# Retention read-out in wide banks, stacked up-projections, grouped transposes and solve, and another order of first loads, in a two-layer hybrid trunk on one core

## Chip, cores and metric

The kernel runs on one core of a Trainium2 chip. The metric is the device time of one execution in microseconds (us), taken as the median of several runs. Beside it there is one execution recorded by the hardware profiler, with the start, the duration and the releaser of each instruction on each engine: PE (TensorE, matmuls and transposes), DVE (VectorE), ACT (ScalarE), POOL (GpSimd), SP (SyncE, which only issues transfers) and the DMA queues.

## What is computed

A decoder trunk of two layers over 512 positions and 1024 channels in float32. In each layer a normalised input is projected at once for three branches and their gates; the branches are merged, projected and added; then comes a gated feed-forward with a causal convolution of width 3.

```python
for l in range(2):
    h = rmsnorm(x, norm1_g[l]);  p = h @ w_in[l]
    p_rw, p_ret, p_sg, gate_logits = split(p, ...)
    # RWKV-7, 8 heads of 64: decay and rate come from two products of rank 64
    w = -softplus(-(w0 + tanh(wd) @ w_up)) - 0.5;  decay = exp(-exp(w));  a = sigmoid(a0 + ad @ a_up)
    S_t = S_{t-1} (diag(decay_t) - kk_t^T (a_t kk_t)) + v_t^T k_t;   y_t = S_t r_t     # then norm, gate
    # retention, 4 heads, 4 chunks of 128, q and k rotated by (cos, sin)
    y_n = (q_n k_n^T * decay_in) v_n + (q_n * q_dec) R_n;  R_{n+1} = R_n chunk_decay + (k_n * k_dec)^T v_n
    y_ret = y / rms(y per head) * silu(g)
    # spatial gating: z = gelu(p_sg), halves u, v;  y_sg = u * (tril(w_s) @ layernorm(v) + b_s)
    x = x + (sum_i sigmoid(gate_i) * (y_i @ w_branch[l, i])) @ w_out[l]
    x = x + conv_ffn(rmsnorm(x, norm2_g[l]))
return rmsnorm(x, final_g)
```

## The kernel before

**Products.** Nearly all work is matmuls of 128x128 weights against 512 columns. A float32 operand is split into two parts of type float32r: hi, a copy on ACT, and lo, what is left, a subtraction on DVE (L127 and L128 for weights, L136 and L137 in `split`). A product is then three matmuls, hi·lo, hi·hi and lo·hi (`mm3`, L144 is its one call of PE). Weights arrive in units of 128x512 (256 KB): `load` issues on SP, `part` splits, and a plan made in a first pass over the program says which unit is next, so that the split runs 2 to 5 units ahead (`AHEAD`). Small products of the branches stay in plain float32.

**Memory.** Tiles of 128x512 come from pools of fixed size in turn: 31 `u`, 16 `r`, 39 `f` (opened in the mixer's second half), and in PSUM two sets of four banks, `acc` for the bulk products and `sm` for everything else. Whoever asks for a fifth `sm` bank waits until the first has been read.

**Order.** The program is emitted in one order and then scheduled; an instruction passed to `keep_in_program_order` (`po`) keeps its place on its engine against the others so marked. Work that is free to be anywhere is held in `fillers`: gates, then the retention's projections `ret_proj`, then half of the gating block's. `fill(n)` emits the next n steps of it, 12 matmuls for a gate's step. `FILL = (33, 3, 1)`: 33 steps ahead of the solve's matmuls, 3 at the start of each of its two groups, 1 at each pause of the recurrence.

**Start (`run`).** All 250 columns of parameters of layer 1 (`load_pc`, 125 KB of them on ACT's queue by the page) are loaded first; then eight blocks of x on SP's queue (two on ACT's), with three weight units between; then a hand-written string of steps: `z` scales and splits a block (L202, L203), `w` splits a weight, `s` squares a block for the norm.

**RWKV (`rwkv`).** `col` finishes a projected row block; `prep(m)` prepares one of four head pairs. In it, L441 multiplies the 64 rows of `w_up` and the 64 rows of `a_up` (both in one tile `wua`, split in hi and lo) by the two halves of `wa`: three matmuls of 64 rows for each, 48 in both layers. `solve` inverts 32x32 triangles: DVE works by rows, then PE makes z (L686) and pt (L694) for the off-diagonal blocks, 16 blocks at a time in two groups, each z copied by ACT (L689) before its pt. L649 and L651 are long diagonal copies on ACT and POOL. The recurrence goes over eight chunks: `vpair` and L551 transpose, L561 and L564 make y and x, L565 and L566 copy x (`XB`), L572 and L574 update, L576 copies on DVE, L581 and L583 finish, L589 or L591 form the next state, which POOL scales (L595). Between the parts stand single filler steps.

**Retention.** In `ret_proj`, run as filler beside the recurrence, each 128 positions of q and k are scaled (L710) and rotated by five DVE operations: one of 512 columns (L716), two products of 256 (L717, L718), a difference and a sum (L719, L720). `ret_heads` transposes them; `ret_chunk(c)` makes scores (L769), masks (L771), read-out (L777, L780) in two banks of two heads each, the mean square of each pair of heads (L786 on DVE, root on POOL in L789), the row scaling (L792), then the next state R (L799 to L807). `ret_out` transposes and splits the result (L815).

**Second half of the mixer.** `sgu_v`, `rwkv_out` and `sgu_bias` run first; L856 sums the masked weights over rows by a float32 matmul with ones. Then comes a hand-written string of steps (L332): S is a gating group (`sgu_out`), R a `ret_chunk`, U two more filler-like steps of the gating projection, Y `ret_out`, and 0, 1, 2 are merges of 12 bulk matmuls each for the three branches (`merge`, L876 to L882; the sum of two branches lies on POOL for 2, on DVE for 1).

**End (`finish`).** The last 256-row weight is multiplied for two halves of 256 positions; for each half the norm's root (POOL) is spread by two transposes (L988), and eight DVE operations of 256 columns (L994) make the output, sent by SP and ACT in turn.

Of the kernel before, what the change touches and what calls it, by code (L numbers as in the profile page):

```python
# [8 lines left out]
F32 = mybir.dt.float32  # L9
# [9 lines left out]
NC = 4  # L19
# [4 lines left out]
FILL = (33, 3, 1)  # L24
# [22 lines left out]
class Emit:  # L47
# [210 lines left out]
    def run(self):  # L258
# [4 lines left out]
        self.ones = self.cp.tile([128, 128], F32, name="ones")  # L263
        V.memset(self.rst, 1.0)
        V.memset(self.ones, 1.0)
        nc.scalar.copy(self.small((128, 1), "ms"), self.rst[:, 0:1])
        wu = self.acc()
        for i in range(6):
            nc.tensor.matmul(wu[:, 0:256], self.rst[:, 0:128], self.rst[:, 256:512], start=True, stop=True)
        self.load_pc(0)  # L270
# [3 lines left out]
        with tc.high_priority():  # L274
            for j in range(8):
# [3 lines left out]
        for step in "z0 w z1 z2 w z3 w z4 z5 w z6 z7 w s0 s1 s2 w s3 s4 s5 s6 s7".split():  # L279
# [9 lines left out]
        self.keep = False  # L289
        tc.keep_in_program_order(nc.scalar.dma_start(self.con, a["con"]))  # L290
# [17 lines left out]
    def mixer(self, l, nst):  # L308
# [20 lines left out]
        self.ret_heads()  # L329
        self.pool = "r"  # L330
        rest, chunk = self.sgu_u(l, range(2, 4)), iter(range(NC))
        for step in "S S 0 0 R U S 0 R 0 U S 0 0 R 0 0 R 2 2 Y 2 1 2 1 2 1 2 1 2 1 2 1 1 1".split():  # L332
            if step == "S":
                ysg.append(self.sgu_out(len(ysg)))
            elif step == "R":
                self.ret_chunk(next(chunk))
# [47 lines left out]
    def rwkv(self, l, nst):  # L384
# [5 lines left out]
        V.tensor_scalar(omu, pcol("mu", 14), -1.0, 1.0, op0=MUL, op1=ADD)  # L390
# [26 lines left out]
        A.activation(wa[0:64, :], wa[0:64, :], AF.Tanh)  # L417
        Xh, Xl = self.split(wa)
# [13 lines left out]
        def prep(m):  # L432
# [5 lines left out]
            for i in range(3):  # L438
                w, x = (Wh, Wh, Wl)[i], (Xl, Xh, Xh)[i]
                for ks, o in ((slice(64, 128), pA), (slice(0, 64), pL)):  # L440
                    T.matmul(o, w[ks, ms], x[ks, :], start=i == 0, stop=i == 2)  # L441
# [99 lines left out]
        for c in range(8):  # L541
# [25 lines left out]
            self.fill(FILL[2], True)  # L567
# [50 lines left out]
    def rwkv_out(self, l, yT, bv, gd):  # L618
# [3 lines left out]
        for m in range(4):  # L622
            ms = slice(m * 128, m * 128 + 128)
            pt = self.sm()
            for c in range(NC):
                T.transpose(pt[:, c * 128:c * 128 + 128], yT[c][:, ms], self.c("ident"))
# [9 lines left out]
    def solve(self, G, n2):  # L636
# [40 lines left out]
        self.fill(FILL[0])  # L677
        for g in range(2):
            self.fill(FILL[1], g > 0)
            us = range(16 * g, 16 * g + 16)  # L680

            zs = self.r((128, 16, 32), n="zs")
            z = [self.sm((128, 16, 32)) for _ in range(2)]
            for i, u in enumerate(us):
                for h in range(2):
                    po(T.matmul(z[h][(hi, lo)[i % 2][h], i, :], G[lo[h], u, 32:64], TD[lo[h], u, :], start=True, stop=True))  # L686
            for h in range(2):
                for e in range(2):
                    A.copy(zs[hi[h], e::2], z[h][(hi, lo)[e][h], e::2])  # L689
            self.fill(FILL[2], True)  # L690
            pt = [self.sm((128, 16, 32)) for _ in range(2)]
            for i, u in enumerate(us):
                for h in range(2):
                    po(T.matmul(pt[h][(lo, hi)[i % 2][h], i, :], zs[hi[h], i, :], TT[hi[h], u, :], start=True, stop=True))  # L694
            for h in range(2):
                for e in range(2):
                    A.copy(G[lo[h], 16 * g + e:16 * g + 16:2, 32:64], pt[h][(lo, hi)[e][h], e::2])
# [425 lines left out]
```

## Time and profile before

| | |
|---|---|
| median of 3 runs | 1767.47 us (1766.63 to 1768.12) |
| profiled execution, whole | 1764.65 us |
| its span on the core | 1762.9 us |
| PE, DVE, ACT, POOL busy | 99%, 66%, 45%, 10% of the span |

Times in the profile are microseconds from the start of the span unless they are marked ns. `L144` is line 144 of the kernel. A line such as `PE sm L574 <- DVE XB L566: a, b, c` in the view of waits gives how often the engine stood idle for that releaser, the sum and the longest of it. In the chain of waits a line has the start, the duration, engine, tile and line, and how many instructions (`x6`) the piece joins. A line of groups has busy time and mean ns of one, then the idle time of the engine ahead of them by what ended it. In a row of the timeline the idle time ahead of an instruction and its releaser stand in brackets. A view by windows gives its length, then for PE, its weight loads, DVE, ACT and POOL the busy time and count, then the granted TensorE clock, the share of the DMA engines and their GB/s.

### The profile page before, as it was taken

The numbers are of one execution on the slowest core, as the hardware profiler recorded it, in microseconds if no ns is written. First come the engines' busy times: TensorE is split into PE (matmuls) and PEld (weight loads), VectorE is DVE, ScalarE is ACT, GpSimd is POOL, SyncE is SP. The second block draws the span as 40 slices with busy tenths as digits, with TensorE's granted clock in tenths as the row PEclk, the third lists the DMA queues.
The fourth block names the chain that finished last, engine by engine and source line by source line (L and its number), as shares of the span: only waits on it lengthen the run. The fifth ranks groups of instructions, "written<-read, shape, count | busy, mean of one in ns | idle before, by whom it ended". The sixth has DMA issues, their size and how long they took to land.

```text
span 1762.9 us, 26337 instructions
## 1 busy us (share of the span) xinstructions
PE 1745.6 (99%) x9870; PEld 1431.8 (81%) x9870; DVE 1163.1 (66%) x1996; ACT 785.8 (45%) x1349; POOL 174.6 (10%) x206
## 2 busy tenths in 40 slices
PE   9999999999999999999999999999999999999998
PEld 7878877888888888888887787778887888888887
DVE  6887746468668777753358876465776687777433
ACT  6564454543244444343245545445332454443321
POOL 0132011013300000000002220110132000000000
PEclk9999999999999999999999999999999999999999
DMA  4224432314442222243322343324154422321332
GB/s 169 78 91 142 140 109 79 123 66 164 161 141 93 97 100 97 68 122 113 111 87 72 117 141 122 104 79 140 60 167 139 150 95 97 100 97 63 111 98 82
DMA packets 104111, 193.30 MB, mean 110 GB/s; under 512 B 11952, under 2 KB 16304, under 8 KB 103984
## 3 DMA queue, kind: packets, MB, share of 16 engines
q1 hardware_dynamic: 89280, 159.42, 28.1%
q10 hardware_dynamic: 10224, 17.52, 2.9%
q0 software_dynamic: 4480, 14.68, 2.5%
q8 instruction: 78, 1.28, 0.3%
q14 instruction: 49, 0.40, 0.1%
HBM read 174.80 MB, written 16.78 MB: 109 GB/s over the span
## 4 chain that ended last, share of the span: by engine, by line
PE 96%; DVE 2%; issue 1%; ACT 1%; DMA 0%; POOLq 0%; POOL 0%; DVEq 0%; ACTq 0%
PE acc L144 88%; PE sm L485 1%; PE sm L441 1%; PE sm L561 0%; PE sm L864 0%; PE sm L780 0%; PE sm L769 0%; PE sm L452 0%; PE sm L564 0%; PE sm L572 0%; PE sm L581 0%; DMA x<-xT 0%; PE sm L144 0%; PE sm L777 0%; PE sm L551 0%
## 5 line engine op out<-in xcount | busy, mean ns | idle before, releaser
L144 PE MATMUL acc<-lo,sh 128*128 128x512 f32 x1056 | 414.2, 393 | 2.2 <-DVE lo L137 1.2
L144 PE MATMUL acc<-hi,sh 128*128 128x512 f32 x1056 | 413.3, 391 | 0.0
L144 PE MATMUL acc<-hi,sl 128*128 128x512 f32 x1056 | 411.6, 391 | 0.0
L127 ACT CAST sh<-wr 128x512 fp32r<-128x512 f32 x376 | 228.3, 612 | 381.8 <-PE acc L144 287.9
L128 DVE TENSOR_TENSOR sl<-wr,sh 128x512 fp32r<-128x512 f32 x376 | 258.5, 691 | 179.9 <-PE acc L144 97.3
L144 PE MATMUL acc<-lo,wh 128*128 128x512 f32 x640 | 253.1, 396 | 1.7 <-DVE lo L203 1.2
L144 PE MATMUL acc<-hi,wh 128*128 128x512 f32 x640 | 250.4, 391 | 0.0
L144 PE MATMUL acc<-hi,wl 128*128 128x512 f32 x640 | 249.5, 391 | 0.0
L128 DVE TENSOR_TENSOR wl<-wr,wh 128x512 fp32r<-128x512 f32 x208 | 150.5, 724 | 131.2 <-ACT wh L127 127.8
L144 PEld LDWEIGHTS acc<-lo,sh 128*128 128x128 f32 x1056 | 198.3, 188 | 45.0 <-issue 3.2
L144 PEld LDWEIGHTS acc<-hi,sl 128*128 128x128 f32 x1056 | 198.3, 188 | 40.7
L144 PEld LDWEIGHTS acc<-hi,sh 128*128 128x128 f32 x1056 | 198.3, 188 | 40.5
L127 ACT CAST wh<-wr 128x512 fp32r<-128x512 f32 x208 | 128.4, 618 | 225.1 <-PE acc L144 193.1
L144 PE MATMUL acc<-ah,sh 128*128 128x512 f32 (+1 forms) x748 | 219.5, 377 | 0.0
L144 PEld LDWEIGHTS acc<-ah,sh 128*128 128x128 f32 x748 | 137.6, 188 | 25.8
L144 PEld LDWEIGHTS acc<-lo,wh 128*128 128x128 f32 x640 | 120.1, 188 | 29.6 <-DVE lo L203 1.9
L144 PEld LDWEIGHTS acc<-hi,wl 128*128 128x128 f32 x640 | 120.1, 188 | 27.0 <-issue 1.1
L144 PEld LDWEIGHTS acc<-hi,wh 128*128 128x128 f32 x640 | 120.2, 188 | 25.4 <-issue 1.1
L144 PE MATMUL acc<-ah,sl 128*128 128x512 f32 (+1 forms) x374 | 140.8, 376 | 0.0
L915 DVE TENSOR_TENSOR fu<-acc,rsF 128x512 f32<-128x512 f32 x88 | 60.7, 690 | 69.6 <-PE acc L144 69.5
L917 ACT ACTIVATE cv<-fu,pc 128x512 f32<-128x512 f32 x88 | 71.8, 816 | 44.0 <-DVE fu L915 39.3
L144 PEld LDWEIGHTS acc<-ah,sl 128*128 128x128 f32 x374 | 70.4, 188 | 12.8
(279 smaller groups left out, 2166.5 us busy)
## 6 DMA issues: line engine op xcount, KB each, us to landing
wr<-wall SPq DMA_DIRECT2D x488, 256.0 KB, 2.6
wr<-wdn SPq DMA_DIRECT2D x80, 256.0 KB, 2.7
gd<-gth ACTq DMA_DIRECT2D x48, 256.0 KB, 3.3
gth<-gd POOLq DMA_DIRECT2D x48, 256.0 KB, 3.2
tab<-rot ACTq DMA_DIRECT2D x8, 256.0 KB, 3.4
xi<-xT SPq DMA_DIRECT2D x8, 256.0 KB, 3.2
wr<-wdn SPq DMA_DIRECT2D x16, 128.0 KB, 2.1
xd<-xi POOLq DMA_DIRECT2D x8, 256.0 KB, 2.8
```

The lines of the kernel that those rows point to most:

```text
L127: self.kept(self.nc.scalar.copy(hi[:, :n], raw[:, :n]))
L128: self.kept(self.nc.vector.tensor_tensor(lo[:, :n], raw[:, :n], hi[:, :n], op=SUB))
L144: i = self.nc.tensor.matmul(*x, **y)
L441: T.matmul(o, w[ks, ms], x[ks, :], start=i == 0, stop=i == 2)
L485: T.matmul(pgs[h][:, j, :], bk[hv[h], c, :, :].rearrange("p a t -> p (a t)"), ag[hv[h], h, c, :], start=True, stop=True)
L915: V.tensor_tensor(u, ps, self.rsF, op=MUL)
L917: A.activation(t, u, AF.Identity, scale=self.p("cw2", j), bias=self.p("cb", j))
```

## The change

It has eight parts, none of which changes the result that is computed.

- **First loads.** The eight columns of the first norm are loaded alone, into a tile of their own, and the whole parameter block after the first string of steps. In that string the fourth block's scaling stands ahead of the second weight's split. One of six warm-up matmuls goes; `ones` becomes float32r and is a copy.
- **Stacked up-projections.** The host stacks `w_up` and `a_up` each upon themselves, so that a weight tile has hi in rows 0 to 63 and lo in rows 64 to 127; the 64 rows of `wa` are doubled likewise, tanh for one and a POOL copy for the other, and split. Two matmuls of 128 rows take the place of three of 64.
- **Solve.** Both groups' z in one run (64 matmuls, each two rows of the trace), both groups' copies, then `FILL[1]` = 2 steps, both groups' pt; DVE makes half of the copies. `FILL` goes from (33, 3, 1) to (36, 2, 1), and the first chunk of the recurrence has one more step behind `XB`.
- **Rotary.** The two products of 256 columns go from DVE to POOL.
- **Retention.** `ret_chunk` becomes `ret_scores` (scores, mask, next state) and `ret_read` (read-out and norm), each in one bank for four heads; the decayed keys `kd` are made in `ret_heads`. In the string of steps `ret_heads` (H) stands behind a merge, scores (K) and read-out (O) are a step or more apart, three merges of branch 0 stand behind the read-out's last, and two behind Y.
- **Transposes in a row.** Those of `rwkv_out`, `ret_heads`, `ret_out` and the matmuls of `sgu_out`, scores and read-out are kept in program order.
- **Ones matmul.** The masked weights are split, and two float32r matmuls take the place of the float32 one.
- **Last rows.** In the second half, three of eight output blocks are scaled by the gain on ACT ahead of time and by the root on POOL; DVE makes five. The broadcast is first copied by ACT for POOL's use.

```diff
-FILL = (33, 3, 1)
+FILL = (36, 2, 1)
...
-        self.load_pc(0)
+        self.pc = self.sp.tile([128, 64], F32, name="g1", tag="g1", bufs=1)
...
+            tc.keep_in_program_order(nc.scalar.dma_start(self.pc[:, 0:8], a["pcols"][0][:, PC["n1"]:PC["n1"] + 8]))
             for j in range(8):
...
-        for step in "z0 w z1 z2 w z3 w z4 z5 w z6 z7 w s0 s1 s2 w s3 s4 s5 s6 s7".split():
+        tc.keep_in_program_order(nc.scalar.copy(self.small((128, 1), "ms"), self.rst[:, 0:1]))
+        tc.keep_in_program_order(nc.scalar.copy(self.ones, self.rst[:, 0:128]))
+        for step in "z0 w z1 z2 z3 w w z4 z5 w z6 z7 w s0 s1 s2 w s3 s4 s5 s6 s7".split():
...
+        self.load_pc(0)
...
+        self.wsp = self.split(self.ws.rearrange("p g i -> p (g i)"), self.f)
...
-        for step in "S S 0 0 R U S 0 R 0 U S 0 0 R 0 0 R 2 2 Y 2 1 2 1 2 1 2 1 2 1 2 1 1 1".split():
+        for step in "0 H 0 S S K 0 U O K U S O K 0 S O K 0 0 O 2 2 Y 0 0 2 1 2 1 2 1 2 1 2 1 2 1 1 1".split():
...
-        wua = self.u(n="wua")
-        self.tc.keep_in_program_order(nc.scalar.dma_start(wua, a["wua"][l]))
-        Wh, Wl = self.split(wua)
+        Ws = []
+        for i in range(2):
+            wua, s = self.u(n="wua"), self.u(dt=F32R, n="wus")
+            self.tc.keep_in_program_order(nc.scalar.dma_start(wua, a["wua"][l, i]))
+            A.copy(s, wua)
+            P.tensor_tensor(s[64:128, :], wua[64:128, :], s[64:128, :], op=SUB)
+            Ws.append(s)
...
-        A.activation(wa[0:64, :], wa[0:64, :], AF.Tanh)
-        Xh, Xl = self.split(wa)
+        Xs = []
+        for i in range(2):
+            x = self.u(n="wax")
+            for h in range(2):
+                o, s = x[64 * h:64 * h + 64, :], wa[64 * i:64 * i + 64, :]
+                if i == 0:
+                    A.activation(o, s, AF.Tanh)
+                else:
+                    P.tensor_copy(o, s)
+            hi, lo = self.u(dt=F32R, n="hi"), self.u(dt=F32R, n="lo")
+            A.copy(hi, x)
+            P.tensor_tensor(lo, x, hi, op=SUB)
+            Xs.append((hi, lo))
...
-            for i in range(3):
-                w, x = (Wh, Wh, Wl)[i], (Xl, Xh, Xh)[i]
-                for ks, o in ((slice(64, 128), pA), (slice(0, 64), pL)):
-                    T.matmul(o, w[ks, ms], x[ks, :], start=i == 0, stop=i == 2)
+            for o, w, (xh, xl) in zip((pL, pA), Ws, Xs):
+                T.matmul(o, w[:, ms], xl, start=True, stop=False)
+                T.matmul(o, w[:, ms], xh, start=False, stop=True)
...
-            self.fill(FILL[2], True)
+            self.fill(FILL[2] + (c == 0), True)
...
         self.fill(FILL[0])
+        zs = [self.r((128, 16, 32), n="zs") for _ in range(2)]
+        z = [[self.sm((128, 16, 32)) for _ in range(2)] for _ in range(2)]
+        for g, i in [(g, i) for g in range(2) for i in range(16)]:
+            for h in range(2):
+                po(T.matmul(z[g][h][(hi, lo)[i % 2][h], i, :], G[lo[h], 16 * g + i, 32:64], TD[lo[h], 16 * g + i, :], start=True, stop=True))
         for g in range(2):
-            self.fill(FILL[1], g > 0)
...
-                    A.copy(zs[hi[h], e::2], z[h][(hi, lo)[e][h], e::2])
+                    (V.tensor_copy if h else A.copy)(zs[g][hi[h], e::2], z[g][h][(hi, lo)[e][h], e::2])
+        self.fill(FILL[1], True)
+        pt = [[self.sm((128, 16, 32)) for _ in range(2)] for _ in range(2)]
...
-            V.tensor_tensor(b[:, :, 0, :], src[:, :, 1, :], Ss, op=MUL)
-            V.tensor_tensor(b[:, :, 1, :], src[:, :, 0, :], Ss, op=MUL)
+            nc.gpsimd.tensor_tensor(b[:, :, 0, :], src[:, :, 1, :], Ss, op=MUL)
+            nc.gpsimd.tensor_tensor(b[:, :, 1, :], src[:, :, 0, :], Ss, op=MUL)
...
+    def ret_scores(self, c):
+        V, T, po = self.nc.vector, self.nc.tensor, self.tc.keep_in_program_order
+        R, v = self.R, self.vt[c]
+        pS = self.sm((128, 4, 128))
+        for j in range(2):
+            po(T.matmul(pS[:, 2 * j:2 * j + 2, :], self.kF[j][:, c, :], self.qB[j][c // 2][:, c % 2], start=True, stop=True))
+        sc = self.u((128, 4, 128), n="sc")
+        V.tensor_tensor(sc, pS, self.c("rmask").rearrange("p (h i) -> p h i", i=128), op=MUL)
+        self.sc, self.Rc = sc, R
...
+    def ret_read(self, c):
+        nc, V, A, T, po = self.nc, self.nc.vector, self.nc.scalar, self.nc.tensor, self.tc.keep_in_program_order
+        R, v, g, sc = self.Rc, self.vt[c], self.yg[c], self.sc
+        hd = [(j, h) for j in range(2) for h in range(2)]
+        pO = self.sm((128, 4, 128))
+        for j, h in hd if c > 0 else ():
+            po(T.matmul(pO[:, 2 * j + h, :], self.qB[j][c // 2][:, c % 2, h, :], R[:, j, :], start=j == h == 0, stop=False, skip_group_check=True))
+        for j, h in hd:
+            i = 2 * j + h
+            po(T.matmul(pO[:, i, :], sc[:, i, :], v[:, 128 * i:128 * i + 128], start=c == i == 0, stop=True, skip_group_check=True))
+        y = self.u((128, 4, 128), n="ry")
+        A.copy(y, pO)
+        sq = self.u((128, 4, 128), n="rsq")
+        A.activation(sq, y, AF.Square)
+        ss = self.small((128, 4), "rss")
+        V.tensor_reduce(ss, sq, axis=AX.X, op=ADD)
+        V.tensor_scalar(ss, ss, 4.0 / 128, 4e-6, op0=MUL, op1=ADD)
+        rr = self.small((128, 4), "rrr")
+        nc.gpsimd.tensor_tensor(rr, ss, self.c("mhalf")[:, 0:4], op=POW)
+        for i in range(4):
+            o = g[:, 128 * i:128 * i + 128]
+            V.scalar_tensor_tensor(o, y[:, i, :], rr[:, i:i + 1], o, op0=MUL, op1=MUL)
...
-        nc.tensor.matmul(pb, self.ones, ws, start=True, stop=True)
+        for i in (1, 0):
+            nc.tensor.matmul(pb, self.ones, self.wsp[i], start=i == 1, stop=i == 0)
...
+            if gx:
+                pbs = self.u((128, 256), n="pbs")
+                po(A.copy(pbs, pb))
+            order = [j for i in range(4) for j in ((i, i + 3) if i < 3 else (6, 7))] if gx else range(8)
...
+                if gx and j < 3:
+                    nc.gpsimd.tensor_tensor(t, gx[j], pbs, op=MUL)
...
-                (nc.sync if j % 2 else nc.scalar).dma_start(self.a["out"][:, j, hs[h]], t)
+                (nc.scalar if j in (1, 4, 6) else nc.sync).dma_start(self.a["out"][:, j, hs[h]], t)
```

More of the change, by code (lines that the diff above doesn't have):

```diff
@@ L262, in run @@
         self.bonesR = self.cp.tile([128, 128], F32R, name="bonesR")
-        self.ones = self.cp.tile([128, 128], F32, name="ones")
+        self.ones = self.cp.tile([128, 128], F32R, name="ones")
         V.memset(self.rst, 1.0)
-        V.memset(self.ones, 1.0)
-        nc.scalar.copy(self.small((128, 1), "ms"), self.rst[:, 0:1])
         wu = self.acc()
-        for i in range(6):
+        for i in range(5):
             nc.tensor.matmul(wu[:, 0:256], self.rst[:, 0:128], self.rst[:, 256:512], start=True, stop=True)
-        self.load_pc(0)
+        self.pc = self.sp.tile([128, 64], F32, name="g1", tag="g1", bufs=1)
         st = self.norm_new()
@@ L760, in ret_heads @@
                 self.kF.append(t)
[L762 to L793 removed]
+        self.kd = []
+        for c in range(NC - 1):
             kd = self.r((128, 4, 64), n="kd")
@@ L960, in finish @@
         hs = [slice(0, 256), slice(256, 512)]
-        pss = [self.acc((128, 256)) for _ in range(2)]
+        pss, gx = [self.acc((128, 256)) for _ in range(2)], []
         def prod(h, k0, k1):
```

97 lines of the change are left out of this document (35 added, 62 removed).

## The prediction

> **What bounds it now.** I read the page first (busy shares, the chain that ended last), then PE's waits, then the chain piece by piece, then DVE, POOL and ACT where the edits lie.
>
> ```profile
> span 1762.9 us, 26337 instructions
> PE 1745.6 (99%) x9870; PEld 1431.8 (81%) x9870; DVE 1163.1 (66%) x1996; ACT 785.8 (45%) x1349; POOL 174.6 (10%) x206
> PE 96%; DVE 2%; issue 1%; ACT 1%; DMA 0%; POOLq 0%; POOL 0%; DVEq 0%; ACTq 0%
> ```
> ```profile
> PE acc L269 <- DVE rst L264: 1.5, 1, 1.5
> PE sm L574 <- DVE XB L566: 1.3, 2, 0.7
> ...
> PE acc L144 <- DVE rst L504: 0.5, 1, 0.5
> ```
> ```profile
> 535.57 350.91 PE acc L144 x1548
> ```
> PE is 96% of the chain, and its ten waits add to 10.5 us (longest and shortest shown). So an edit counts if it takes PE issue time away or moves a wait of PE; work taken from DVE or ACT counts only through such a wait. A bulk matmul (L144, 128x512) costs 350.91/1548 = 0.227 us from start to start; the busy means of 0.39 us overlap and are no price.
>
> **The decay and rate projections (L441).** 48 half-height matmuls (64 rows) become 32 of full height.
>
> ```profile
> 41.44 0.89 PE sm L441 x6
> ...
> 997.32 0.90 PE sm L441 x3
> ```
> ```profile
> 93.78 0.39 PE L144 MATMUL acc<-lo,wh 128*128 128x512 f32 x1
> 94.09 0.50 PE L441 MATMUL sm<-lo,hi 64*128 64x512 f32 x1
> ...
> 94.98 0.50 PE L144 MATMUL acc<-hi,wh 128*128 128x512 f32 x1
> 95.32 0.40 PE L144 MATMUL acc<-hi,wl 128*128 128x512 f32 x1
> ```
> From 93.78 to 95.32 stand two bulk matmuls and three halves: 1.54 - 2 x 0.227 = 1.09 us for three, the turn between shapes included. Six in turn cost the same (x6, 0.89): two halves overlap when neighbours, and only two of the eight groups are so. The chain shows two of x6 and ten of x3 (first and last above); the last six stand in smaller pieces. 12 x 1.09 + about 1.5 = 14.6 us. After: 32 x 0.227 = 7.3, in the bulk matmul's own shape. **-7.3 us**.
>
> ```profile
> 11.40:147.70 136.30, 136.30 (x706) 110.23 (x707) 109.39 (x177) 81.04 (x139) 25.76 (x19) 1.00 0.31 102
> ```
> In these 136 us of layer 1 PE is never idle and DVE is busy for 80% (109.39; ahead of it PE and its weight loads, behind it ACT and POOL). The doubled operands cost ACT, POOL and a DMA, but the first projection now stands 84 bulk matmuls (19 us) behind the row transposes instead of 50, which covers the longer preparation; without that cover it would be POOL's four new pieces, at the prices below some 5 us, once a layer.
>
> **The ones matmul (L856)** goes from float32 to two float32r.
>
> ```profile
> 366.56 0.86 PE sm L856 x2
> ```
> 0.86 a layer becomes 2 x 0.227: **-0.8** for both. Its split lies on ACT and DVE four steps earlier.
>
> **The triangular solve.** Two groups become one; behind z stand two filler steps instead of one, 24 bulk matmuls, 5.4 us.
>
> ```profile
> 205.79 0.39 PE L144 MATMUL acc<-hi,wl 128*128 128x512 f32 x1
> 206.11 0.75 PE L686 MATMUL sm<-cs,GB 32*32 32x32 f32 x64
> 206.79 0.50 PE L144 MATMUL acc<-lo,wh 128*128 128x512 f32 x1
> ...
> 209.74 1.20 PE L694 MATMUL sm<-cs,zs 32*32 32x32 f32 x64
> ...
> 1077.08 0.85 PE L686 MATMUL sm<-cs,GB 32*32 32x32 f32 x64 [0.70 <-DVE cs L671]
> ...
> 1080.49 0.39 PE L144 MATMUL acc<-hi,wl 128*128 128x512 f32 x1
> 1081.37 0.24 PE L694 MATMUL sm<-cs,zs 32*32 32x32 f32 x2 [0.49 <-ACT zs L689]
> 1082.14 1.09 PE L694 MATMUL sm<-cs,zs 32*32 32x32 f32 x62 [0.53 <-ACT zs L689]
> 1083.17 0.50 PE L144 MATMUL acc<-lo,wh 128*128 128x512 f32 x1
> ```
> ```profile
> 1078.82 1.05 ACT GB L649
> ```
> A stretch of 64 takes 0.68 and 0.2 for the two turns (0.09 ahead, as at 206.11; 0.11 behind, as at 95.32): joining saves 0.2, twice a layer, **0.8** in all. Of the waits, L686's 0.70 stays: ahead of z stand 36 filler steps, as the 33 and 3 before. L694 waits 0.45 in layer 1 (1.20 beside 0.75) and 1.7 in layer 2 (2.68 from 1080.49 to 1083.17, where 205.79 to 206.79 is 1.00), because ACT copies z behind two long copies (L649). Now 24 matmuls cover it and DVE copies half; but in layer 2 two casts and two tanhs, 2.5 us, stand on ACT behind L649 and ahead of z, so I keep 0.5 of that wait: **1.65** gained. New: pt fills all four sm banks when the next transposes ask for one; they wait for two ACT copies (0.36 each), partly beside pt, 0.5 a layer: **1.0** lost. Together **-1.5 us**; bounds -2.9 (no bank wait, no backlog) and +0.5 (ACT's casts in front everywhere).
>
> **The rotary half on POOL (L717, L718).** 16 DVE operations go to POOL. DVE is in order, and queued behind its sums (L719, L720), which now wait for POOL, is the copy L576 of the recurrence, for which PE waits.
>
> ```profile
> 429.74 1.28 POOL L882 TENSOR_TENSOR gth<-gth,gth 128x512 f32<-128x512 f32 x1 [3.63 <-DVE gth L879]
> 430.29 1.28 DVE L128 TENSOR_TENSOR sl<-wr,sh 128x512 fp32r<-128x512 f32 x1 [0.64 <-ACT sh L127]
> ...
> 434.18 0.68 DVE L128 TENSOR_TENSOR sl<-wr,sh 128x512 fp32r<-128x512 f32 x1
> ```
> ```profile
> L595 POOL TENSOR_TENSOR fS<-cs,F 64x256 f32<-64x256 f32 x24 | 15.0, 624 | 146.9 <-DVE cs L591 89.4 <-DVE cs L589 56.5
> ```
> ```profile
> 281.09 0.69 DVE L716 TENSOR_TENSOR ro<-qs,tab 128x512 f32<-128x512 f32 x1 [0.44 <-ACT qs L710]
> 281.70 0.42 DVE L717 TENSOR_TENSOR rb__558_2936<-qs,tab 128x256 f32<-128x256 f32 x1
> ```
> One of 256 columns is 0.42 on DVE and, by L595 and by half of 1.28, 0.64 on POOL. And L128, 0.68 alone, takes 1.28 when a POOL operation that reads SBUF is running: it ends 0.55 after POOL does. The two take turns. In the changed order L576's copy stands behind two products (0.69 each), three sums, a part subtraction, a third product and a fourth sum, which need four POOL results. In turns, each after the other's end (POOL 0.53, DVE 0.54 or 0.28), I get 6.2 us from the first product to the copy's end, 5.1 after the last matmul of the projection (the first product starts 1.1 ahead of it, as at 281.09). PE's cover is 0.83 for pu and 2.72 for a filler, 3.55: PE waits about 1.6, and about 0.8 more at the next chunk's state copy, which stands behind the other four POOL products. Now it waits about 1.0 there (L574 on XB, behind the same rotary work: 0.65 each in the waits, which count from a matmul's modelled end, 0.16 after the next could have started, and a turn). So +1.4 a layer, **+2.8**. Bounds: with no turns DVE has 4.4 us of work before the copy and PE nothing to wait for, -2.0; if all eight products take turns ahead of the copy it ends 8.3 after, +7.7.
>
> The Trainium skill speaks against this edit: "SBUF — State Buffer", section "Who interferes with whom", states that a DVE instruction with two SBUF inputs and a GpSimd instruction that reads SBUF exclude each other for the whole instruction. The rows agree as far as they go; taken to the letter for all eight products it gives the upper bound, and without it the lower.
>
> **Read-out, scores and gating block.** Merging two banks into one leaves PE's rows as many and as wide; a turn between float32 and bulk matmuls in the 128-row shape costs little. It shortens DVE: 8 masks and 8 reductions of 0.42 become 4 of 0.69 each, and eight small operations go, 1.8 us a layer.
>
> ```profile
> 379.80:437.20 57.40, 57.21 (x313) 48.98 (x311) 46.99 (x106) 24.44 (x50) 14.79 (x21) 1.00 0.41 138
> ```
> ```profile
> L128 DVE TENSOR_TENSOR sl<-wr,sh 128x512 fp32r<-128x512 f32 x19 | 13.5, 716 | 7.0 <-issue 3.0 <-PE acc L144 2.3 <-ACT sh L127 1.5
> ...
> L792 DVE SCALAR_TENSOR_TENSOR sgg<-ry,rrr,sgg 128x128 f32<-128x128 f32 x16 | 5.9, 409 | 0.6 <-POOL rrr L789 0.6
> ```
> ```profile
> 437.62 0.50 PE L144 MATMUL acc<-lo,sh 128*128 128x512 f32 x1 [0.61 <-DVE lo L137]
> ```
> But from the head transposes to the last output transposes (379.8 to 437.2) stand 164 bulk matmuls now and 114 after: 11.3 us less for PE, while DVE's 47.0 lose only the 1.8 and four steps' worth (two operations of 0.7 each), 40 of 46 us, 88% instead of 82%. Added row by row, with the part subtractions that run ahead, DVE needs 46 us between the first head copy and the last row scaling, PE 42. PE would meet the mask of chunk 3 about 1.2 late and the last scaling 0.5 late: +1.7 a layer. The wait at 437.62 (about 1.0 a layer with its lead, as the merge that needs the transposes now comes three merges later) and split transposes (0.4) go. **+0.6** for both layers; bounds -2.8 (no new wait) and +13 (DVE takes 46 us plus its waits for POOL's roots, 8 a layer).
>
> **First loads and last rows.**
>
> ```profile
> pc<-pcols ACTq DMA_DIRECT2D x1, 125.0 KB, 4.3
> ...
> 5.86 0.72 ACT L202 ACTIVATE hi<-x,pc 128x512 fp32r<-128x512 f32 x1 [3.56 <-DMA pc<-pcols]
> 9.13 0.60 ACT L127 CAST wh<-wr 128x512 fp32r<-128x512 f32 x1
> ...
> 11.37 0.50 PE L144 MATMUL acc<-lo,wh 128*128 128x512 f32 x1 [0.27 <-DVE lo L203]
> ...
> 1756.42 3.22 DVE L994 SCALAR_TENSOR_TENSOR o<-xi,pc,sm 128x256 f32<-128x256 f32 x8 [1.30 <-PE sm L988]
> ```
> PE runs without a gap from 11.37, when the fourth x block is ready. That block is now scaled ahead of the second weight's cast (0.60), and 125 KB of columns leave the front of the queues (0.4 at the 269 GB/s of the first 14 us): **-1.0**. It may shrink to 0: on POOL the first norm's root now stands behind two splits that wait for a second weight load. At the end eight DVE operations of 0.40 become five, with three on POOL: POOL ends 0.37 (a copy) + 3 x 0.64 after the broadcast, about 0.8 ahead of DVE's 3.22 now, and SP issues one more after it: **-0.4**.
>
> **Sum.** -7.3 - 0.8 - 1.5 + 2.8 + 0.6 - 1.0 - 0.4 = -7.6 us, against the profiled run's 1764.65 (1762.9 span and 1.7 around it), which lies 2.8 under the median of the runs: 1767.47 - 7.6 = 1759.9.
>
> **Rivals.** (a) The rotary work on POOL disturbs nothing: 4.8 less, 1755. For it: POOL is 10% busy. Against: the 1.28 rows. 13%. (b) All eight products take turns: +4.9, 1765. For it: 1.28; against: the second table lands late, as its load is issued after the first two products. 12%. (c) The projection gain is not kept, because DVE at 80% paces the casts there: without the 7.3 it is 1767. Against: PE has no wait there now. 10%. (d) Slower: DVE paces the read-out. The compressed stage has 8 us a layer too little at the upper bound instead of 1.7, so +12.6, 1772.5; it comes out slower than now from 5.5 us a layer. For it: the 88%, and in-order rows that wait for POOL's roots; against: the part subtractions are taken ahead. 15%. The forecast keeps 50%, with its own range of 1754 to 1765.
>
> **Range and chances.** The low end takes (a) and the solve's and read-out's lower bounds, 1750; the high end most of (d), 1770. A difference under 0.2% (3.5 us) I call none. Faster: the forecast's 0.45, (a) 0.13, part of (b) 0.05: 0.63. Same: the rest of the forecast and of (b) and most of (c): 0.21. Slower: (d) and a little of (c), 0.16.
>
> **What would show it.** L441's successors in chain pieces with bulk matmuls, no 0.09 us turn around them; L686's as one stretch of 128; in the rotary stretch POOL and DVE rows longer than 0.64 and 0.69, and a PE wait of 1 to 3 us ahead of the second half of the state update; DVE near 90% in the read-out; PE's bulk run starting near 10.3. It is wrong if PE's waits grow by more than 8 us, or if the halves' successors cost more than 0.23 each.

## The result, and the profile after

The median is 1771.74 us (1770.93 to 1775.47, 7 runs) against 1767.47: a ratio of 1.0031, 95% interval 1.0021 to 1.0041. The change makes the kernel 5.5 us slower, where 7.6 us less were forecast. The profiled execution took 1770.93 us.

First lines and chain of the page of after:

```profile
span 1769.2 us, 26290 instructions
PE 1741.3 (98%) x9852; PEld 1436.5 (81%) x9852; DVE 1170.8 (66%) x1966; ACT 781.7 (44%) x1330; POOL 203.7 (12%) x229
PE 91%; DVE 5%; ACT 2%; issue 1%; POOL 0%; POOLq 0%; ACTq 0%; DVEq 0%
```

PE is busy 4.3 us less, and DVE and ACT now hold 7% of the chain. The view of PE's waits says where (its longest entries; the last two shown stand at the start and at the end of the program, as before):

```profile
PE acc L144 <- DVE wl L128: 7.2, 7, 2.1
PE sm L602 <- DVE cs L597: 4.1, 2, 2.6
PE sm L519 <- ACT ag L510: 1.5, 2, 0.8
PE sm L552 <- ACT GB L717: 1.4, 2, 0.7
PE acc L144 <- ACT wh L127: 0.7, 2, 0.4
...
PE acc L267 <- DVE rst L264: 1.5, 1, 1.5
PE sm L1015 <- POOL rs L1009: 1.1, 1, 1.1
```

In all PE's waits add to 19.9 us, 9.4 more than before. The first line is new: bulk matmuls wait for the split of a weight, seven times, all of them in the stretches of the decay preparation. The second is the update of the recurrence behind the rotary work. The old waits for split transposes and for merged sums are gone.

To see all that was won and lost, each execution is cut at the same matmuls, and from each piece 0.2267 us is taken for each bulk matmul in it; what is left is small matmuls, waits and slow matmuls. The table gives the difference to the execution of before in us (layer 1 / layer 2), worked out from the start times in the traces. It adds up to the spans (+6.3 for after).

| piece | after | e1, no stacking | e3, rotary on DVE | e7, without the three |
|---|---|---|---|---|
| first 200 bulk matmuls | -2.0 | -1.5 | -0.8 | -0.4 |
| decay preparation | +5.7 / +3.1 | 0.0 / 0.0 | +5.8 / +3.4 | 0.0 / 0.0 |
| ahead of z | 0.0 / -0.8 | 0.0 / 0.0 | 0.0 / -0.8 | 0.0 / 0.0 |
| solve | -0.2 / -1.5 | -0.2 / -1.1 | -0.2 / -1.5 | -0.2 / -1.2 |
| recurrence | +3.0 / +2.1 | +4.9 / +2.5 | +0.5 / +0.5 | +0.4 / +0.5 |
| up to the ones matmul | -0.1 / -0.1 | +0.3 / -0.1 | -0.1 / -0.1 | +0.5 / -0.1 |
| read-out and merges | -2.2 / -2.6 | -2.2 / -2.6 | -2.2 / -2.6 | -2.2 / -2.6 |
| end | +1.8 | +1.5 | +1.5 | -0.3 |

How a wait for a split comes about shows in the timeline of DVE, after, layer 2 (L476 to L495 belong to one decay preparation):

```profile
975.22 1.04 DVE L128 TENSOR_TENSOR wl<-wr,wh 128x512 fp32r<-128x512 f32 x1
976.19 1.38 DVE L476 TENSOR_SCALAR cs<-cs 128x512 f32<-128x512 f32 x1
977.60 1.23 DVE L477 TENSOR_TENSOR_SCAN cs<-rst,cs 128x512 f32<-128x512 f32 x1
...
983.42 1.51 DVE L491 SCALAR_TENSOR_TENSOR ag<-rwc,pc,cs 64x512 f32<-64x512 f32 x2
984.96 0.17 DVE L486 TENSOR_TENSOR F<-F,cs 128x7 f32<-128x7 f32 x1
985.05 0.69 DVE L128 TENSOR_TENSOR wl<-wr,wh 128x512 fp32r<-128x512 f32 x1
```

and before, where a split stands in the middle of the same preparation:

```profile
948.80 0.67 DVE L471 SCALAR_TENSOR_TENSOR cs<-cs,rwc 128x512 f32<-128x512 f32 x1
...
950.07 0.69 DVE L128 TENSOR_TENSOR wl<-wr,wh 128x512 fp32r<-128x512 f32 x1
950.88 1.51 DVE L474 SCALAR_TENSOR_TENSOR bk<-cs,nkk,cs 64x512 f32<-64x512 f32 x2
...
953.90 1.51 DVE L470 SCALAR_TENSOR_TENSOR ag<-rwc,pc,cs 64x512 f32<-64x512 f32 x2
955.44 0.69 DVE L128 TENSOR_TENSOR wl<-wr,wh 128x512 fp32r<-128x512 f32 x1
```

A split feeds 12 bulk matmuls, 2.7 us, and splits run two units ahead. A gap of 5.4 us between two of them (950.07 to 955.44) is covered; one of 9.8 (975.22 to 985.05) is not. L476 takes 1.38 here, while POOL masks the preparation ahead of it, and 0.41 where POOL is idle. What it does to PE, in PE's timeline:

```profile
983.71 0.40 PE L144 MATMUL acc<-hi,wh 128*128 128x512 f32 x1
985.79 0.80 PE L144 MATMUL acc<-hi,wl 128*128 128x512 f32 x1 [1.68 <-DVE wl L128]
986.38 0.63 PE L144 MATMUL acc<-lo,wh 128*128 128x512 f32 x1
986.81 0.63 PE L144 MATMUL acc<-hi,wh 128*128 128x512 f32 x1
987.24 0.63 PE L144 MATMUL acc<-hi,wl 128*128 128x512 f32 x1
```

Behind the wait the matmuls start 0.43 us apart instead of 0.227. The view by windows gives the granted clock (the number behind POOL's count) for this place and behind the rotary wait of layer 1:

```profile
290.00:292.00 2.00, 2.00 (x10) 1.63 (x10) 2.00 (x3) 1.01 (x3) 1.93 (x3) 1.00 0.43 134
296.00:299.00 3.00, 3.00 (x11) 2.38 (x8) 2.94 (x6) 0.73 (x2) 0.92 (x2) 0.50 0.00 0
986.00:987.00 1.00, 1.00 (x3) 0.81 (x4) 1.00 (x3) 0.63 (x1) 0.00 (x0) 0.50 0.26 66
1170.00:1173.00 3.00, 3.00 (x9) 2.35 (x8) 2.97 (x5) 0.00 (x0) 1.76 (x3) 0.50 0.00 0
```

It is halved behind the waits; the last row is the rotary wait of layer 2. So a wait is paid a second time: these slow matmuls cost 1.6 us behind a wait in the first stretch, 1.4 in the second, and 1.6 and 1.4 behind the two rotary waits, 6.0 in all in this execution, nearly as much as the 6.3 by which its span is longer. Between 20 and 1745 us the execution of before has none of them. The mean granted clock says the same of the other runs: 0.993 to 0.995 in the seven of the changed kernel, 0.997 in the median run of the kernel before, whose runs at 0.999 took 1764.9 us on average and those at 0.995 1769.4.

### The profile page after: what moved, and what is told of

It reads as the page before. It is cut to its first block, busy times and chain, and to the rows that moved or that the text cites. A ratio compares the mean times of both kernels' runs of the same rounds, so it can differ in the third digit from the quotient of the medians.

```text
span 1769.2 us, 26290 instructions
## 1 busy us (share of the span) xinstructions
PE 1741.3 (98%) x9852; PEld 1436.5 (81%) x9852; DVE 1170.8 (66%) x1966; ACT 781.7 (44%) x1330; POOL 203.7 (12%) x229
## 4 chain that ended last, share of the span: by engine, by line
PE 91%; DVE 5%; ACT 2%; issue 1%; POOL 0%; POOLq 0%; ACTq 0%; DVEq 0%
PE acc L144 84%; DVE wl L128 1%; PE sm L582 0%; PE sm L506 0%; PE sm L602 0%; PE sm L822 0%; PE sm L891 0%; ACT ag L510 0%; PE sm L794 0%; DVE ag L491 0%; PE sm L585 0%; DVE bk L495 0%; PE sm L593 0%; DVE cs L477 0%; ACT GB L509 0%
## 5 line engine op out<-in xcount | busy, mean ns | idle before, releaser
L128 DVE TENSOR_TENSOR sl<-wr,sh 128x512 fp32r<-128x512 f32 x376 | 253.7, 678 | 186.6 <-PE acc L144 91.1
L128 DVE TENSOR_TENSOR wl<-wr,wh 128x512 fp32r<-128x512 f32 x208 | 155.6, 749 | 126.1 <-ACT wh L127 124.9
```

The source lines that it names most:

```text
L128: self.kept(self.nc.vector.tensor_tensor(lo[:, :n], raw[:, :n], hi[:, :n], op=SUB))
```

## The experiments

All times are medians; the ratio is to the kernel before, run beside it, with its interval. Differences between two kernels are differences of ratios times 1767.4 us; with intervals of about 0.001 on each side, such a difference is uncertain by some 2.4 us.

**e1, no stacking** (undoes the stacked weights and operands, and the product):

```diff
-            for o, w, (xh, xl) in zip((pL, pA), Ws, Xs):
-                T.matmul(o, w[:, ms], xl, start=True, stop=False)
-                T.matmul(o, w[:, ms], xh, start=False, stop=True)
+            for i in range(3):
+                w, x = (Wh, Wh, Wl)[i], (Xl, Xh, Xh)[i]
+                for ks, o in ((slice(64, 128), pA), (slice(0, 64), pL)):
+                    T.matmul(o, w[ks, ms], x[ks, :], start=i == 0, stop=i == 2)
```

> Only the stacked up-projections are undone: 48 matmuls of 64 rows again, their preparation as before. Theory: the stacking shifts the decay preparation against the weight splits on DVE, the gap between two splits grows to 6.4 to 9.8 us, and PE waits for a split (7.2 us in the waits, 5.7 and 3.1 us in the two stretches). Then those waits go, and the time falls by about 8.8, to 1763. Rival: another part of the change (the order of the first loads, POOL's other work) brings the waits; then they stay, PE has 4.5 us more rows of its own, and the time is 1772 to 1776. Second rival: DVE was at its limit there and only kept PE from gaining; then the time stays within 1 us of 1771.7.

1764.79 us, 0.9989 (0.9981 to 0.9998): 7.4 us less than the change. No wait for a weight split is left in its list, and both stretches are as before to 0.01 us:

```profile
PE sm L588 <- DVE cs L583: 5.1, 2, 3.1
PE sm L538 <- ACT GB L703: 1.7, 2, 1.0
PE acc L267 <- DVE rst L264: 1.5, 1, 1.5
```

**e2, stacking alone** (the same edit the other way, on the kernel before).

> The kernel before with the stacked up-projections and nothing else of the change. Theory: the same waits for weight splits appear, about +8.8, 1776; the gap between splits in the second layer reaches some 10 us. The prediction's sum would give 1767.5 - 7.3 = 1760. Its rival (c), gain not kept, 1767.

1771.13, 1.0025 (1.0016 to 1.0034): +4.4. The stretches are +5.8 and +3.1 us, as in the change, and the waits for splits 7.3. The rest comes back in layer 2's solve (-2.1): PE arrives later there, so it no longer waits for DVE. So the stacking alone brings the loss; the size expected, +8.8, was too large, in part by that.

**e3, rotary products on DVE**

```diff
-            nc.gpsimd.tensor_tensor(b[:, :, 0, :], src[:, :, 1, :], Ss, op=MUL)
-            nc.gpsimd.tensor_tensor(b[:, :, 1, :], src[:, :, 0, :], Ss, op=MUL)
+            V.tensor_tensor(b[:, :, 0, :], src[:, :, 1, :], Ss, op=MUL)
+            V.tensor_tensor(b[:, :, 1, :], src[:, :, 0, :], Ss, op=MUL)
```

> The changed kernel with the two rotary products back on DVE. Theory: the two waits at the state update (2.6 and 1.5 us) go, the two of 0.65 for the copy of x come back: the time falls by 2 to 3, to 1769. Rival: the waits come from the recurrence's extra step and order, not from POOL; then the time stays at 1771.7 or rises with DVE's load.

1768.28, 1.0012 (1.0003 to 1.0021): 3.4 us less. The wait in the recurrence falls from 4.1 in two (up to 6.2 in other executions with POOL's products) to 2.0 in four, none over 0.7, and no matmul behind them is slow. By the pieces this is worth 4.1 us, of which the slow matmuls behind the two rotary waits are 3.0. In the change, DVE's and POOL's timelines show the two taking turns:

```profile
289.50 0.96 DVE L739 TENSOR_TENSOR ro<-ro,rb__568_3000 128x256 f32<-128x256 f32 x1
...
293.87 0.94 DVE L740 TENSOR_TENSOR ro<-ro,rb__571_3009 128x256 f32<-128x256 f32 x1
294.84 0.43 DVE L597 COPY cs<-sm 64x256 f32<-64x256 f32 x1
```
```profile
288.99 1.19 POOL L738 TENSOR_TENSOR rb__568_3000<-qs,tab 128x256 f32<-128x256 f32 x1
290.13 0.92 POOL L737 TENSOR_TENSOR rb__571_3009<-qs,tab 128x256 f32<-128x256 f32 x1
```

**e4, last rows as before** (`finish` of the kernel before).

> The changed kernel with the last rows as before (eight operations on DVE, none on POOL). Theory: POOL's closing drain ends 4.7 us after its last operation in both kernels, and is the last thing that ends now; without the products on POOL it hides again: -1.8, 1770. Rival: the loss is DVE's late start behind ACT's copy of the broadcast; then only 0.4 comes back, 1771.3, and POOL's drain still ends last.

1770.34, 1.0020 (1.0011 to 1.0029): 1.9 us less, which alone is not clear of the noise. The traces are: the piece "end" stands at +1.5 to +1.8 in all 11 executions with the new last rows, and at -0.5 to +0.2 in the 8 with the old ones. The closing instructions of after and of before, per line count, shortest, median and longest in ns, then first and last start:

```profile
L1153 POOLq DRAIN  x3: 40/102/6786, 1761.6 to 1768.9; - x3
```
```profile
L1114 POOLq DRAIN  x3: 40/93/5396, 1755.2 to 1762.4; - x3
```

POOL's long drain ends at 1768.4 in after and 1760.6 before: 4.67 us after POOL's last operation, here as there, and 4.66 to 4.67 in all 20 executions. Before, it hid behind DVE's eight operations and their transfers; now the last thing computed is on POOL, and the drain ends 1.5 us after everything else.

**e5, preparation on DVE** (stacked; the `P.tensor_tensor` and `P.tensor_copy` of the preparation become `V.`).

> The changed kernel, stacked as it is, but the four pieces of its preparation that lay on POOL (two subtractions for the weights, the copy of 64 rows, two subtractions for the operands) lie on DVE. The program's order on DVE then has fewer operations between two weight splits (no gap with more than 5 us of DVE work, where the changed kernel has one of 10). Theory (the waits come from where the decay preparation falls between the weight splits, which the late preparation on POOL decides): waits for a split fall from 7.2 to under 2 us and the time to 1763 to 1765. Rival (DVE is full there, whatever the order): the added 3 us of DVE work a layer makes the waits longer, 1774 or more.

1769.84, 1.0016 (1.0007 to 1.0025): 2.7 us less, about a third of what the order theory wanted, and the waits for splits do not fall (7.7 in five). The stretch of layer 2 falls from +3.1 to +1.0, 1.4 of it because no slow matmul follows a wait there; that of layer 1 stays (+5.3), with one wait of 3.4 and 13 slow matmuls behind it. The order and the engine of the preparation have a share, but do not explain layer 1.

**e6, splits three units ahead** (`AHEAD` None: 3, four pairs of buffers, 29 tiles `u`).

> The changed kernel with weight splits of this stage running three units ahead instead of two (a fourth pair of buffers, two fewer general tiles). Theory: one more unit covers 2.7 us of a late split, so the waits of up to 2.1 us for splits mostly go: the time falls by 5 to 8, to 1764 to 1767. Rival (DVE has too much work in the stretch): a deeper buffer only delays the waits, and the time stays within 2 us of 1771.7.

1771.85, 1.0027 (1.0016 to 1.0038): no gain. Waits for splits fall from 7.2 to 1.4, but in the preparation PE then waits 4.7 for ACT's copies out of PSUM (L510), so that the stretches still stand at +2.5 and +1.9, and the start stands at +4.5 with a wait of 3.6 for the first norm's root on POOL. (The profiled execution, 1776.07, is the longest of the seven.) The buffer moved the wait.

**e9, late halves** (e1, but the operands of the half-height products are copied and split on POOL):

```diff
-        Xh, Xl = self.split(wa)
+        Xh, Xl, wc = self.u(dt=F32R, n="hi"), self.u(dt=F32R, n="lo"), self.u(n="wax")
+        P.tensor_copy(wc, wa)
+        A.copy(Xh, wc)
+        P.tensor_tensor(Xl, wc, Xh, op=SUB)
```

> The changed kernel with half-height projections again (as e1), but the 64+64 rows of their operand are copied and split on POOL, so that the first projection stands 84 bulk matmuls behind the row transposes, as in the changed kernel, and not 50. No rows are saved. If the late place alone brings the waits for weight splits (it packs four preparations into a shorter stretch): waits of 3 to 7 us and a time of 1768 to 1772, well above e1's 1764.8. If the waits need PE's shorter rows (PE asks for splits sooner than DVE, loaded at 80%, makes them): no wait for a split over 0.5 us and a time within 1 us of 1764.8.

1770.77, 1.0021 (1.0012 to 1.0030). No wait for a split in the two stretches (one of 0.8 elsewhere), which stand at +1.2 and -0.4: the late place alone does not starve PE there. But the time is not e1's: the solve of layer 1 is 3.9 us longer, by a wait of 2.5 inside z that the profile puts down to no releaser, and slow matmuls behind it. What that wait is stays open; in the trace a 16 KB transfer of instructions starts at 207.50, just as PE stops (207.49), but nothing shows that PE waits for it.

**e10, e13, e14, e18: one DVE operation less, and a confounder.** e10 moves one operation of each preparation to ACT:

```diff
+        ceh = self.small((128, 1), "ceh")
+        P.memset(ceh, -0.5 * EXP_HALF)
...
-            V.tensor_scalar(ld, ld, -0.5 * EXP_HALF, -0.5 * EXP_HALF, op0=MUL, op1=ADD)
+            A.activation(ld, ld, AF.Identity, scale=-0.5 * EXP_HALF, bias=ceh)
```

> The changed kernel with one DVE operation of each decay preparation (the scale and shift after tanh, 0.41 us alone and 1.38 beside POOL, four in each layer) on ACT. If the stretch lacks DVE time between two splits: DVE loses 3 us in each stretch, the waits for splits fall from 7.2 to 2 to 4 us, and so does the reduced clock behind the longest; time 1766 to 1768. If it is only the order in which splits stand: no change beyond 1 us.

1771.31, 1.0026 (1.0016 to 1.0035): on its face nothing. But both stretches are shorter (+1.6 and +1.2), and pieces that the edit doesn't touch are longer, 1.5 and 1.2 us in the two feed-forwards alone. e13 gives the tile 64 bytes (`(128, 16)`, one buffer), e14 has only tile and memset, e18 only a wider tile:

```diff
-        omu = self.small((128, 14), "omu", bufs=1)
+        omu = self.small((128, 32), "omu", bufs=1)[:, 0:14]
```

> As e10, but the one new small tile takes 64 bytes instead of twice 4, so that the tiles placed behind it stand at the same offset modulo 64 as in the changed kernel. In e10 the two stretches of the decay preparation were 6.1 us shorter than in the changed kernel, but bulk matmuls in the merges and the feed-forward took 229 to 235 ns instead of 227, 5.1 us in all. If the offset does that: 1771.3 - 5.1 = 1766, with the stretches as in e10. If moving the operation to ACT does it: 1771 again.

> The changed kernel with the unused small tile of e10 (twice 4 bytes) and its memset, and nothing else. If the offset of the tiles behind it slows the matmuls: bulk intervals of 229 to 235 ns in merges and feed-forward and 5.1 us more, 1777. If not: 1771.7.

> The changed kernel with one small tile of 14 columns widened to 32, which no instruction reads or writes: only the addresses of the tiles behind it move. If the address is what slows the matmuls in e14: intervals of 229 to 235 ns in the merges and the feed-forward, and 1775 to 1777. If it is the memset (another instruction on POOL): 1771.7.

1770.64, 1.0025 (1.0016 to 1.0035); 1777.38, 1.0051 (1.0037 to 1.0066); 1777.09, 1.0067 (1.0053 to 1.0081). e14 and e18 are the change made about 4 and 6 us slower by columns that nobody uses; e18 has the same instructions as the change, so it is the addresses. The bulk matmuls with the activations as moving operand show it; 560 to 860 us of after, then of e18:

```profile
L144 PE MATMUL acc<-ah,sh x287: 389/389/389, 762.7 to 859.9; 128*128 128x512 f32 x144
```
```profile
L144 PE MATMUL acc<-ah,sh x281: 387/394/397, 763.5 to 859.8; 128*128 128x512 f32 x141
```

About 1800 of 6869 intervals between bulk matmuls are 229 to 235 ns instead of some 390 of them. Against its proper control e14, e10 gains 4.4 us and e13 4.6 (0.0026): by the pieces of e13 +5.7 becomes +1.5 in layer 1 and +3.1 becomes +1.1 in layer 2. Of these 6.1 us, 3.1 are slow matmuls that are gone and 2.4 are shorter waits in the two stretches. The waits for splits still add to 7.2, not the 2 to 4 expected, but none is over 1.6 and no matmul behind them is slow. So less DVE work between the splits helps (the gaps of 6.4 to 9.8 us become 5.9 to 7.7), more by keeping the waits short than by ending them; that DVE time is all that lacks is not shown. That offset modulo 64 does the slowing is refuted (e13 has it too); which property of the address does is open.

**e12, read-out as before** (`ret_heads`, `ret_chunk` and the string of steps of the kernel before).

> The changed kernel with the retention's heads, read-out and the string of steps as before. The stages of the profile give the new read-out 2.2 and 2.6 us (read-out and the merges behind it), so its undoing costs 4.8: 1776.5. The prediction's sum gave the new read-out +0.6, and its rival (d) a loss; by these the time would stay or fall, 1771 or less.

1778.02, 1.0058 (1.0045 to 1.0070): 4.8 us more. The waits that the new order removes come back:

```profile
PE acc L144 <- DVE lo L137: 1.4, 2, 0.7
```

**e7, without the three losing parts; e8, e11, e15, e17: with stacking kept.** e7 is e1, e3 and e4 in one. The others keep the stacking but neither of the other two: e8 has e5's preparation; e11 copies the operands on ACT, splits them on DVE and has e10's edit; e15 is e11 with e13's tile; e17 has an immediate instead (`AF.Copy, scale=-0.5 * EXP_HALF, bias=-0.5 * EXP_HALF`). e16 is e7 with e13's edit, without stacking.

> The changed kernel without the stacking, with the rotary products on DVE and with the last rows as before. By the single runs (1.0031 against 0.9989, 1.0012 and 1.0020) the three give 7.4, 3.4 and 1.9: 1767.5 + 5.5 - 12.7 = 1760. Rival: they share a wait (PE arrives earlier at the solve, where it waits 0.7 to 2 for DVE), then 1762.

> The stacking with its preparation on DVE, the rotary products on DVE and the last rows as before. Theory: as e7, less what the stacked rows save (4.5 us of PE rows in the two profiles, up to 7 with the turns): 1755 to 1757. Rival: no gain over e7, 1760, since DVE now paces the stretch.

> The stacking with the weights split on POOL, the operands copied on ACT and split on DVE (so that the first projection stands 60 bulk matmuls behind the row transposes), the scale and shift on ACT, the rotary products on DVE and the last rows as before. If DVE time was what lacked, waits for splits are under 2 us and the row saving of about 3 us a layer is kept: 1752 to 1755, under e7's 1758.2. If PE's saving only turns into waits: 1758 to 1763.

> As e11 with the 64-byte tile. If the offset cost e11 the same 5 us: 1757.5, about e7's 1758.2, as its two stretches (0.2 us above before each) are no shorter than e7's: the row saving then turns into waits for splits and nothing is won by stacking. If stacking helps: 1755 or less.

> e7 with the scale and shift on ACT and the 64-byte tile. PE has no wait for splits in e7, so DVE time freed there is worth nothing: 1758 within 1 us, unless the solve starts earlier in layer 2 (0.7 us of wait ahead of z).

> As e15, but the scale and shift on ACT take their constant as an immediate, so that there is neither the small tile nor its memset. If these two cost e15 the 5 us that they cost the changed kernel in e14: 1757.5, within 1.5 us of e7's 1758.2. If stacking with a relieved DVE is worth the 3 us a layer of its rows: 1752.

| | median | ratio | 95% interval |
|---|---|---|---|
| e7 | 1758.22 | 0.9949 | 0.9937 to 0.9962 |
| e8 | 1762.73 | 0.9974 | 0.9964 to 0.9985 |
| e11 | 1762.50 | 0.9977 | 0.9968 to 0.9986 |
| e15 | 1762.56 | 0.9972 | 0.9962 to 0.9983 |
| e16 | 1763.90 | 0.9979 | 0.9970 to 0.9988 |
| e17 | 1758.80 | 0.9955 | 0.9944 to 0.9967 |

e7 beats both kernels, by 9 us the one before. e17, whose preparation is early and whose DVE is relieved, only equals it: its stretches stand at +0.8 and +0.3, with waits for splits of

```profile
PE acc L144 <- DVE wl L128: 5.1, 3, 2.5
```

In e8, e11 and e15 these waits are 7.7, 4.4 and 4.2, where under 2 was hoped for in e11. e16 is e7 made 5.7 us slower, with the tile's 1800 slow intervals, and e15 lies 1.3 us under it with the same handicap, which is not clear of the noise. So within what was tried, rows saved in this stretch turn into waits; no gain from stacking is shown.

## Why the prediction was wrong, step by step

**The projections (-7.3): the step that failed.** Their matmuls did get shorter: the rows of L441 took 11.8 us, those in their place 7.3, and the turns between shapes went. But the text took PE's gain for the kernel's, because PE had no wait there and DVE was busy for 80%, and it gave the longer preparation and the later place of the products no price, as covered. Undone, they give 7.4 us back (e1). Two things stand in its place. The first is waits: PE stands idle for 9.5 us in the two stretches, where it never did before, and with the saved rows already in them the stretches are 8.8 us longer. PE without a wait at 80% on DVE was near its limit: splits run two units, 5.4 us, ahead, and gaps of 5.1 to 6.3 us full of DVE work stood in the profile before; in the change they are 6.4 to 9.8 us. Why they grew is shown in part only: e10 and e13 show that less DVE work between the splits helps, e5 that the order and the engine of the preparation have a share, e9 that the late place alone does not bring the waits; that PE's faster rows and POOL's operations beside L476 and L128 are the rest is argued. The second is the clock: 3.1 of the 8.8 us are matmuls at half clock behind two of the waits, which the prediction did not know. Rival (c), "the projection gain is not kept, because DVE at 80% paces the casts there", had the mechanism and too mild a price: zero gain, 1767. The prediction's own sign of being wrong, waits that grow by more than 8 us, came true with 9.4.

**The rotary half (+2.8): the wait right, the size in part by luck.** 3.4 by e3. The wait stood where it was put, ahead of the second half of the state update, behind the fourth sum and L597's copy (L576 before). A turn of POOL and DVE was priced at 0.81 to 1.07 us; POOL's products start 0.89 to 1.15 apart. But the waits are only 2.1 us more than with the products on DVE (4.1 against 2.0), and 3.0 of the cost are slow matmuls behind them, which were no term of the sum. The rows bear out the rule of the Trainium skill ("SBUF — State Buffer", section "Who interferes with whom") that the two exclude each other; the upper bound of +7.7, with all eight products ahead of the copy, was not reached.

**The read-out (+0.6): mis-sized, and rival (d) with it.** It is -4.8 by e12. No wait of PE is left in that stretch, though DVE is as full as was said:

```profile
392.10:433.00 40.90, 40.90 (x235) 36.00 (x234) 36.62 (x79) 19.54 (x36) 7.04 (x9) 1.00 0.40 126
```
```profile
398.33 0.68 DVE L895 TENSOR_TENSOR sgm<-sgm,sgu 128x512 f32<-128x512 f32 x1
398.94 0.68 DVE L796 TENSOR_TENSOR sc<-sm,con 128x512 f32<-128x512 f32 x1
399.54 0.68 DVE L895 TENSOR_TENSOR sgm<-sgm,sgu 128x512 f32<-128x512 f32 x1
```

The 46 us added up DVE's durations, and these overlap: rows of 0.68 start 0.60 apart. From the first head copy to the last row scaling it took 42.4 us, idle time included, although the durations in it add to 43.6. PE's intervals had been taken start to start, DVE's not. So the +3.4 of new waits for both layers did not come. The old waits went: those for parts (L137 in the list of before, 1.2 us) had been counted, those for sums in the merges (L879, 1.0) had not. What makes up the rest beyond the lower bound of -2.8 was not separated.

**The solve (-1.5): right.** -0.2 and -1.5 in the table, and the wait for two ACT copies ahead of the next transposes (L552 on L717) is the 0.7 a layer, 0.5 forecast. The 0.7 ahead of layer 2's z went only because PE came late; in e7 it is back.

**Ones (-0.8): right**, two rows of 0.23 instead of 0.86 a layer. **First loads (-1.0): right within its spread**, -0.4 to -2.0 in 16 of the 18 executions with the new start. In e6 and e11 it stands at +4.5 and +1.3, with waits of 3.6 and 2.7 for the first norm's root on POOL, the danger that the prediction named.

**Last rows (-0.4): failed, +1.9.** DVE's operations were counted, the closing of the program not: POOL's drain. The sign rests on the traces, as said at e4.

Sum by the experiments: stacking +7.4, rotary +3.4, end +1.9, read-out -4.8 make +7.9; what is left to the +5.5, -2.4, is the start, the solve and the ones matmul, forecast at -3.3.

## What to carry to other kernels

A stage in which PE never waits can still be close to starving: look at the longest gap between the operations that feed it and at how far these run ahead, not at the feeding engine's busy share (90% without a wait in the read-out, 82% with 5 us of them in layer 1's preparation). Add up start-to-start intervals for every engine, not durations. And a wait of about 2 us may be paid twice, and what ran last on POOL here was paid with its drain.

## What was not expected of the hardware

- **Waits that halve the clock.** In the 20 profiles, between 20 and 1745 us, 12 of 14 waits of PE of 2.7 us and more were followed by bulk matmuls at 0.43 us, for 1.9 us of extra time on average (up to 2.8), 18 of 31 between 1.6 and 2.7, and 3 of 31 between 0.8 and 1.6. The Trainium skill, "TensorE: Matmul & The Clock Gate", section "HAM oscillation — how this bites in real kernels", warns of idle gaps over some 3.4 us; here shorter ones suffice, though not each time. The traces' records of the clock bear on why: it changes only at instants whole multiples of 3.413 us apart (in the change at 135.35, 138.76, 295.78, 299.19, 985.27, 988.68, 1169.59 and 1173.00). With PE's idle time added up in each window between such instants, half clock followed on all 29 windows at full clock with 1.89 us idle or more, on 4 of 17 with 1.48 to 1.83, and on none of 179 with 0.3 to 1.48. By these records it matters where a wait falls and what other waits share its window; no experiment moved a wait to test this.
- **Addresses that slow matmuls.** One small tile wider by 18 columns, 72 bytes in a partition, costs about 5 us (e18), with no instruction changed. An experiment that adds a tile needs a control that has the tile alone.
- **POOL's drain** ended 4.66 to 4.67 us after POOL's last operation in all 20 profiles, be it the norm's root (2 columns) or an output product (256 columns).
